# Two modulation chunks moved into the first full gate tile, and the finish of each chunk set ahead of other work

## The chip, the cores and the metric

The kernel runs on one core of a Trainium2 chip. The metric is the device time of one execution in microseconds (us). TensorE (PE) does the matrix products, VectorE (DVE), ScalarE (ACT) and GpSimd (POOL) the elementwise work, and SyncE (SP) issues the loads. Each engine, SP too, works through its own list of instructions in order, so what waits holds up what stands behind it in that list.

## The reference, cut to what matters

A two-layer backbone over 256 latent tokens and 256 context tokens, width 2048, all in float32. Layer 0 mixes by pooling, layer 1 by neighbourhood attention; each layer ends in a gated MLP with a width-3 convolution of the gate (5504 hidden columns). Every sub-layer is modulated by vectors worked out from `silu(c)` and `silu(c_ctx)`:

```python
ml = (silu_c @ w_mod[i] + b_mod[i]).reshape(B, 6, 1, D)       # six vectors of 2048
a_lat = modulate(rms_norm(h, norm1_g[i]), ml[:, 0], ml[:, 1])  # shift, scale of the mixer
h = h + ml[:, 2] * y_lat                                       # gate of the mixer
h = h + ml[:, 5] * conv_ffn(modulate(rms_norm(h, norm2_g[i]), ml[:, 3], ml[:, 4]), ...)
```

The last of the six (`ml[:, 5]`) is only used where the output of the MLP's down product is added to `h`.

## The kernel before, in words

**Products.** A float32 weight is split into a high and a low part (`split`, lines 135 to 151: ACT casts the high part at L147, DVE subtracts at L149), and an activation likewise, and three products hi·hi, hi·lo, lo·hi are summed in PSUM. Each product has 512 columns: 256 of the latent and 256 of the context stream.

**Loads.** `load` (L125) brings weights in pieces of 128 x 1024 values, 512 KB each, into staging slots that `stage` (L115) takes in rotation from the list `rooms`. There are six slots of their own (`wst1` to `wst6`); while the tiles of the activation `A` are not yet written, `lend` adds some of them to the list. A slot can be loaded again when the last instruction that reads its old piece is done: the split for an ordinary weight, the product itself for a modulation weight, which is used unsplit. After layer 0's partial sums `rooms` is cut to slots 1, 2 and 3 (L670, L671), because slots 4 to 6 serve layer 1's modulation weights (`mod_pairs`).

**Modulation of layer 0.** The six vectors are made in 24 chunks of 512 columns (chunk 4w+q is quarter q of vector w; chunks 20 to 23 are the MLP's output gate). `mod_pe` (L195) does one chunk in four steps, one step for each 512 rows of `w_mod`: two loads of 512 KB and eight small products into the PSUM bank "m" (L206); I call such a step a quarter, 22.0 for step 0 of chunk 22, and 22.0a and 22.0b its two loads (columns 0 to 1023 and 1024 to 2047 of the piece). After the fourth step ACT copies the bank to SBUF (L219, `modev`), PE transposes it (L224, `modt`, at high priority), DVE sums the four row groups (L226) and `finish_mod` adds the bias (L189). These last parts run when the generator is asked for the following step. `need(n)` (L487) runs steps until n are done, 96 and an end in all. `shifts(g)` (L470) copies the finished shift vector of group g to where PE multiplies it by the weights (L583).

**Stages of layer 0.** After the mixer of group g, `partial(g)` (L565) multiplies group g (512 of 2048 rows) of the MLP's first eight gate and up tiles (`cg`, `cu`), and the function `between` (L640), called 32 times in each `partial`, asks for modulation steps at a set rate. In `partial(3)` it also normalises the tiles A0 to A11 for the remaining gate tiles and starts the gates 0 to 3. Then come gate 6, A12 to A15, and `gu0(8)`: the first gate and up tile over the whole width (96 products `g`, `u`, L687 to L689). `down0(0)` follows (L697): the down product of hidden tiles 0 to 3, 16 output tiles of 12 products each (`d`, L713 to L715), for which `wd` is loaded in eight pieces. Each output tile is scaled by the output gate (L725) and added to `h` by GpSimd. From there PE goes on with gate tiles and down products without a break to the end of the layer.

**Order.** The program is written in one sequence; a scheduler sets each engine's order by a simulated timeline and by priority, and `tc.high_priority()` puts what is inside it ahead of other work that is ready. PSUM banks: four for `gu`, three for `d`, one for `m`. `bank` (L71) can place every fourth "d" tile in "m" once `nbank[0]` is set, which happens when all modulation steps are done (L662, L663):

```python
            need(97)
            nbank[0] = 0
            A.update(F)
```

Of the kernel before, what the change touches and what calls it, by code (L numbers as in the profile page):

```python
# [13 lines left out]
ALU = mybir.AluOpType  # L14
AX = mybir.AxisListType
# [15 lines left out]
NS = 8  # L31
NC = 6

LEAD = 18
RATE = 20
PMAX = 30

NRH = 3
GATES = (16, 19, 22, 25)
# [20 lines left out]
def kernel(ctx: ExitStack, tc: tile.TileContext, xT, cxT, wmod, wg, wu, wd, wp,  # L60
                         wq, wv, wo, vec, cc, rope, inv, strips, out):
    nc = tc.nc
# [6 lines left out]
    nbank = [None]  # L69

    def bank(tag, name):  # L71

        if tag == "d" and nbank[0] is not None:
            nbank[0] += 1
            if nbank[0] % 4 == 0:
                tag = "m"
        return pp.tile([P, 512], F32, tag=tag, bufs={"gu": 4, "d": 3, "m": 1}[tag], name=name)
# [8 lines left out]
    def V(name):  # L86
        a, b = _OFF[name]
        return vt[:, a:b]
# [22 lines left out]
    def lend(ks):  # L111

        rooms[:] = [r for r in rooms if r < 0 or r in ks] + [k for k in ks if k not in rooms]
# [11 lines left out]
    def load(src, cols, name):  # L125

        ts = []
        for j in range(0, cols, 1024):
            n = min(1024, cols - j)
            t = stage(f"{name}_{j}")  # L130
            fetched.append(nc.sync.dma_start(t[:, :n], src(j, j + n)).ins)
            ts.append((t, n))
        return ts
# [19 lines left out]
    def ld(src, name, share=0):  # L153
        return split(load(lambda a, b: src[:, a:b], 2048, name), name, share)


    modT = {}

    both = (0, 1)

    def mod_tile(l, ch):

        return main.tile([P, 4, 2], F32, tag=f"modT{ch if ch < 20 else (l, ch)}", name=f"modT{l}_{ch}")

    def by_row(ps):

        return ps.rearrange("p (i j c) -> p i c j", i=4, j=4)[:, :, 0:2, :]
# [9 lines left out]
    def finish_mod(l, ch, streams, src):  # L177

        mt = src[0] if len(src) == 1 else mod_tile(l, ch)
        n = len(streams)  # L180
        which, q = divmod(ch, 4)

        def dup(name, a):
            return V(name)[:, a : a + 8].rearrange("p (i s) -> p i s", s=2)[:, :, 0:n]

        bias = dup(f"bm_{l}", 8 * ch)
        for b, v in enumerate(src):
            own = slice(32 * b, 32 * b + 32) if len(src) > 1 else slice(0, P)
            nc.vector.tensor_tensor(mt[own, :, 0:n], v, bias[own], op=ALU.add)  # L189
        if which in (1, 4):  # L190
            nc.vector.scalar_tensor_tensor(mt[:, :, 0:n], mt[:, :, 0:n], 1.0, dup(f"g{1 if which == 1 else 2}_{l}", 8 * q),
                                           op0=ALU.add, op1=ALU.mult)
        modT[l, ch] = mt

    def mod_pe(l, ch, sc, pool):  # L195

        ps = bank("m", f"mod{l}_{ch}")
        held = []
        for g in range(4):
            ts = load(lambda a, b: wmod[l, ch, g, :, a:b], 2048, f"wm{l}_{ch}_{g}")  # L200
            held.append((g, ts, fetched[-2:]))
            if ch > 20 or g % 2:
                with ExitStack() as behind:
                    for n, (gg, tt, _) in enumerate(held[::-1]):
                        for j in (2, 3, 0, 1):
                            ins = nc.tensor.matmul(ps[32 * j : 32 * j + 32, :], sc[:, 4 * gg + j, :],  # L206
                                                   tt[j // 2][0][:, 512 * (j % 2) : 512 * (j % 2) + 512],
                                                   start=(g < 2 and (n == 0 and held[0][0] == 0)),
                                                   stop=(g == 3 and gg == held[0][0]), tile_position=(0, 32 * j))
                            if n == 0 and j == 2:  # L210
                                for x in sum((d for _, _, d in held), []):
                                    tc.add_manual_dep(ins.ins, x.name, mybir.DependencyInfo(
                                        mybir.DependencyClass.Sync, mybir.DependencyReason.DATA), reason="whole")
                                behind.enter_context(tc.issue_after(ins.ins))
                                behind.enter_context(tc.high_priority())
                held = []
            if g == 3:
                ev = pool.tile([P, 512], F32, tag="t2", name=f"modev{l}_{ch}")
                nc.scalar.copy(ev, ps)  # L219
            yield  # L220
        with tc.high_priority():
            p2 = bank("d", f"modt{l}_{ch}")
            for i in range(4):
                nc.tensor.transpose(p2[:, P * i : P * i + P], ev[:, P * i : P * i + P], ident)  # L224
        r = mod_tile(l, ch)
        nc.vector.tensor_reduce(out=r, in_=by_row(p2), axis=AX.X, op=ALU.add)  # L226
        finish_mod(l, ch, both, [r])

    def mod_pairs(todo, ring):

# [143 lines left out]
    chunks = [list(range(f, min(f + 4, NF))) for f in range(0, NF, 4)]  # L374
# [3 lines left out]
    with ExitStack() as ph0:  # L378
# [58 lines left out]
        acts = {}  # L437
# [3 lines left out]
        with ExitStack() as phs:  # L441
# [20 lines left out]
            shs = []  # L462
# [6 lines left out]

            def shifts(g):  # L470
                READY.add(g)
                nc.vector.tensor_copy(shs[g % 2][:, :, 0:2], modT[0, 12 + g])

            def mods():

# [9 lines left out]
            done = [0]  # L485

            def need(n):  # L487
                while done[0] < n:
                    next(pump0, None)
                    done[0] += 1  # L490
# [140 lines left out]
            for g in range(4):  # L631
                if g < 3:
                    lend((range(8, KT), [*range(12, KT), *range(4)], range(8))[g])
                mix = mixer(g + 1) if g < 3 else None
                todo = [20 * g + 20 + n for n in STEPS] if g < 3 else []
                last = [14]
                F = {}
                rstd = n2.acc

                def between(half):  # L640
                    need(min(20 * g + LEAD + RATE * (half + 1) // 32, 20 * g + LEAD + PMAX))
                    if (g, half) in LENT:
                        lend(LENT[g, half])
                    if g == 3 and half == NRH:
                        nc.scalar.copy(rstd, n2.rstd())
                        late_norm.append(rstd)
                    if todo and done[0] > todo[0] and half >= last[0] + 2:
                        last[0] = half
                        todo.pop(0)
                        next(mix)  # L650
                    k = (half - NRH) // 2
                    if g == 3 and 0 <= k < 12 and (half - NRH) % 2 == 0:
                        normalise(0, 3, h_of, both, rstd, f0, range(k, k + 1), keep=F)
                    if g == 3 and half in GATES:
                        e = GATES.index(half)
                        acts[e], _ = gate0(e, *late(e))

                partial(g, shs[g % 2], between)
                for n in todo:
                    need(n)  # L660
                    next(mix)
            need(97)  # L662
            nbank[0] = 0  # L663
            A.update(F)

        whx = ph0.enter_context(tc.tile_pool(name="whx", bufs=1, reuse_waits="tile"))
# [6 lines left out]
        one = [(1, q, 2, (0,)) for q in range(8, 24, 2)]  # L673
        pump = mod_pairs([x for t in zip(two, one) for x in t], ring)

        def gu0(f):
            res = []
            for nm, wsrc in (("g", wg), ("u", wu)):
                parts = ld(wsrc[0, f], f"w{nm}0_{f}")
                if f > NS + 3:  # L680
                    next(pump, None)
                ps = bank("gu", f"{nm}0_{f}")
                for k in range(KT):
                    hi, lo = parts[k // 8]
                    c = P * (k % 8)
                    xh, xl = flat(A[k][:, 0]), flat(A[k][:, 1])
                    nc.tensor.matmul(ps, hi[:, c : c + P], xh, start=(k == 0), stop=False)  # L687
                    nc.tensor.matmul(ps, hi[:, c : c + P], xl, start=False, stop=False)  # L688
                    nc.tensor.matmul(ps, lo[:, c : c + P], xh, start=False, stop=(k == KT - 1))  # L689
                    if k == 7 and f > NS + 3:  # L690
                        next(pump, None)
                res.append(ps)
            return res

# [36 lines left out]
        normalise(0, 3, h_of, both, rstd, f0, range(12, 14))  # L731
        acts[NC], sg = gate0(NC, *r6)
        normalise(0, 3, h_of, both, rstd, f0, range(14, KT))
        res = gu0(NS)
        rest = [e for e in range(NS) if e not in acts]

        def more():
            e = rest.pop(0) if rest else None
            if e is not None:
                acts[e], _ = gate0(e, *late(e))  # L740

        while rest and rest[0] < 4:
            more()
        down0(0, chunks[0], [acts[f] for f in chunks[0]], more)
        while rest:
            more()
        acts[NS], sg = gate0(NS, *res)
# [42 lines left out]
    with ExitStack() as ph2:  # L790
# [164 lines left out]
        for c, fs in enumerate(chunks):  # L955
            acts = []
# [404 lines left out]
```

## Time and profile before

| what | value |
|---|---|
| median of 3 executions | 3050.64 us (3046.84 to 3052.1) |
| the profiled execution | 3052.48 us, its span 3050.7 us |
| PE busy | 2976.8 us, 98% of the span |
| DVE, ACT, POOL busy | 64%, 45%, 28% |
| mean DMA rate | 184 GB/s |
| mean granted TensorE clock | 0.992 |

A row of the timeline reads: start, duration, engine, line, operation, output <- inputs, shape, count; in brackets the idle time of the engine before it and what ended it. Names lose their numbers, so `mod<-wm` is any modulation product and `cu<-Ad` any partial up product; `SPq` rows are load issues. A row of the waits reads: who, for what; us in total, times, longest. A row of the stages reads: stage, its length, then busy us and count of each engine, granted clock of PE, DMA share, GB/s. A row of the DMA issues ends with the median us from the issue to the landing.

### The profile page before, as it was taken

To read this page: it belongs to the slowest core of one execution; us is meant where nothing else is said; L and a number is where in the kernel's file an instruction comes from. 1 tells how busy PE (TensorE), PEld (TensorE's weight loads), DVE (VectorE), ACT (ScalarE), POOL (GpSimd) and SP (SyncE) were. 2 spreads that over 40 slices of the span, in tenths; PEclk is the share of its full clock that TensorE was granted. 3 is DMA by queue.
4 is the path that set the end of the run, shared out by engine and by line. 5 is a ranking of instruction groups with operands and counts; after the bars stand their busy time and mean duration, and the time that the engine had idled before them with its cause. 6 is when DMAs were issued, how large, how long until landed. Compare 5 with 4: busy or idle time off the path is not lost.

```text
span 3050.7 us, 40962 instructions
## 1 busy us (share of the span) xinstructions
PE 2976.8 (98%) x15092; PEld 2416.8 (79%) x15092; DVE 1949.0 (64%) x2765; ACT 1377.7 (45%) x2237; POOL 849.4 (28%) x840
## 2 busy tenths in 40 slices
PE   5999999999999999999999999999999999999998
PEld 2666668888888888888887888878788888888887
DVE  4455764386574857658485666474778666666666
ACT  4333454323333242333334444343556666666665
POOL 2111313303122030311312001020002566566665
PEclk9999999999999999999999999999999999999999
DMA  9888663384665747566482333343346655555563
GB/s 392 328 305 313 218 208 98 104 255 142 216 189 170 235 149 237 154 205 211 148 256 75 114 108 110 110 128 103 110 155 194 192 187 193 189 184 187 183 198 110
DMA packets 178503, 561.80 MB, mean 184 GB/s; under 512 B 17664, under 2 KB 22272, under 8 KB 178304
## 3 DMA queue, kind: packets, MB, share of 16 engines
q1 hardware_dynamic: 178304, 559.19, 56.2%
q8 instruction: 119, 1.95, 0.2%
q14 instruction: 80, 0.66, 0.1%
HBM read 557.03 MB, written 2.10 MB: 183 GB/s over the span
## 4 chain that ended last, share of the span: by engine, by line
PE 91%; DMA 3%; DVE 3%; POOL 1%; issue 1%; ACT 1%; SPq 0%; DVEq 0%; POOLq 0%; ACTq 0%
PE g L882 5%; PE u L882 5%; PE d L713 5%; PE d L714 5%; PE d L715 5%; PE d L935 4%; PE g L687 4%; PE g L689 4%; PE g L688 4%; PE u L688 4%; PE u L689 4%; PE u L687 4%; PE g L885 3%; PE u L885 3%; PE d L939 2%; PE mod L206 2%
## 5 line engine op out<-in xcount | busy, mean ns | idle before, releaser
L726 POOL TENSOR_TENSOR hl<-hl,dy 128x256 f32<-128x256 f32 x160 | 146.3, 914 | 942.1 <-ACT dy L725 941.9
L950 POOL TENSOR_TENSOR hl<-hl,dy 128x256 f32<-128x256 f32 x320 | 332.1, 1074 | 188.3 <-ACT dy L948 186.0
L262 DVE SCALAR_TENSOR_TENSOR macc<-wm,sc,macc 128x512 f32<-128x512 f32 (+1 forms) x360 | 328.8, 944 | 67.5 <-DMA wm<-wmod 66.7
L725 ACT ACTIVATE dy<-d,modT 128x256 f32<-128x256 f32 x320 | 133.0, 469 | 187.7 <-PE d L715 171.8
L726 POOL TENSOR_TENSOR hc<-hc,dy 128x256 f32<-128x256 f32 x160 | 129.5, 809 | 0.0
L948 ACT ACTIVATE dy<-d,modT 128x512 f32<-128x512 f32 x160 | 104.6, 684 | 42.9 <-PE d L939 41.3
L149 DVE TENSOR_TENSOR wd_2l<-wd,wd_2h 128x1024 fp32r<-128x1024 f32 (+1 forms) x44 | 54.6, 1246 | 108.2 <-ACT wd_2h L147 106.9
L206 PE MATMUL mod<-wm,sc 128*32 128x512 f32 x768 | 98.3, 633 | 9.7 <-DMA wm<-wmod 8.1
L1037 POOL TENSOR_TENSOR rk<-rk,rp 128x256 f32<-128x256 f32 x16 | 15.1, 944 | 330.6 <-DVE rk L1036 237.5
L149 DVE TENSOR_TENSOR wd_3l<-wd,wd_3h 128x1024 fp32r<-128x1024 f32 (+1 forms) x44 | 52.0, 1202 | 77.9 <-ACT wd_3h L147 76.5
L149 DVE TENSOR_TENSOR wd_1l<-wd,wd_1h 128x1024 fp32r<-128x1024 f32 (+1 forms) x44 | 53.7, 1224 | 60.8 <-ACT wd_1h L147 60.8
L521 POOL TENSOR_TENSOR pf<-ws,inv 128x256 f32<-128x256 f32 x32 | 29.4, 939 | 212.2 <-DVE ws L516 149.8
L147 ACT CAST wd_1h<-wd 128x1024 fp32r<-128x1024 f32 (+1 forms) x44 | 45.3, 1032 | 81.4 <-PE u L688 56.9
L149 DVE TENSOR_TENSOR wd_0l<-wd,wd_0h 128x1024 fp32r<-128x1024 f32 (+1 forms) x44 | 54.5, 1247 | 37.3 <-ACT wd_0h L147 37.3
L147 ACT CAST wd_0h<-wd 128x1024 fp32r<-128x1024 f32 (+1 forms) x44 | 45.2, 1032 | 56.0 <-PE u L882 29.1
L1126 ACT ACTIVATE sb<-sb,nm 128x512 f32<-128x512 f32 x64 | 46.1, 721 | 52.7 <-DVE nm L1122 52.2
L914 DVE TENSOR_TENSOR actb<-sgb,actb 128x256 fp32r<-128x256 f32 x43 | 51.4, 1195 | 26.0 <-ACT actb L913 26.0
L206 PEld LDWEIGHTS mod<-wm,sc 128*32 128x32 f32 x768 | 21.7, 113 | 57.8 <-issue 55.1
L713 PE MATMUL d<-act,wd_2h 128*128 128x512 f32 x172 | 67.1, 390 | 0.0
L715 PE MATMUL d<-act,wd_2l 128*128 128x512 f32 x172 | 66.9, 389 | 0.0
L714 PE MATMUL d<-act,wd_2h 128*128 128x512 f32 x172 | 66.9, 389 | 0.0
L715 PE MATMUL d<-act,wd_0l 128*128 128x512 f32 x172 | 66.9, 389 | 0.0
(1750 smaller groups left out, 9312.7 us busy)
## 6 DMA issues: line engine op xcount, KB each, us to landing
wm<-wmod SPq DMA_DIRECT2D x384, 512.0 KB, 6.1
wd<-wd SPq DMA_DIRECT2D x168, 512.0 KB, 4.5
wg<-wg SPq DMA_DIRECT2D x156, 512.0 KB, 4.6
wu<-wu SPq DMA_DIRECT2D x156, 512.0 KB, 4.6
wv<-wv SPq DMA_DIRECT2D x32, 512.0 KB, 4.2
wk<-wq SPq DMA_DIRECT2D x32, 512.0 KB, 4.1
wq<-wq SPq DMA_DIRECT2D x32, 512.0 KB, 4.0
wo<-wo SPq DMA_DIRECT2D x32, 512.0 KB, 4.4
```

What stands on the lines that cost most here:

```text
L149: eng.tensor_tensor(lo[:, :n], t[:, :n], hi[:, :n].bitcast(F32), op=ALU.subtract)
L262: nc.vector.scalar_tensor_tensor(acc[s], v, sc2[:, k, s : s + 1], acc[s], op0=ALU.mult, op1=ALU.add)
L687: nc.tensor.matmul(ps, hi[:, c : c + P], xh, start=(k == 0), stop=False)
L688: nc.tensor.matmul(ps, hi[:, c : c + P], xl, start=False, stop=False)
L689: nc.tensor.matmul(ps, lo[:, c : c + P], xh, start=False, stop=(k == KT - 1))
L713: nc.tensor.matmul(ps, hi[:, o : o + P], xh, start=(i == 0), stop=False)
L714: nc.tensor.matmul(ps, hi[:, o : o + P], xl, start=False, stop=False)
L715: nc.tensor.matmul(ps, lo[:, o : o + P], xh, start=False, stop=(i == n - 1))
L726: nc.gpsimd.tensor_tensor(h_of(s)[:, k, :], h_of(s)[:, k, :], y[:, s], op=ALU.add)
L882: nc.tensor.matmul(ps, hi[:, c : c + P], flat(B[k]), start=(k == 0), stop=False)
L885: nc.tensor.matmul(ps[:, T:], lo[:, c : c + P], B[k][:, 0], start=False, stop=(k == KT - 1))
L950: nc.gpsimd.tensor_tensor(hl[:, k, :], hl[:, k, :], y[:, q], op=ALU.add)
```

## The change

- In `mod_pe` ACT's copy `modev` and DVE's sum and `finish_mod` go under `tc.high_priority()`, and so does the copy in `shifts`.
- A constant `LAST = 88` stops the modulation steps in `partial(3)` after 22 of the 24 chunks. The remaining eight steps (chunks 22 and 23) run inside `gu0(8)`: after every fourth of the 16 row tiles of g and of u one step is asked for. The end of chunk 23 (transpose, sum, bias) is asked for after the first four output tiles of `down0(0)`, and only there `nbank[0]` is set.

```diff
             if g == 3:
                 ev = pool.tile([P, 512], F32, tag="t2", name=f"modev{l}_{ch}")
-                nc.scalar.copy(ev, ps)
+                with tc.high_priority():
+                    nc.scalar.copy(ev, ps)
...
-        r = mod_tile(l, ch)
-        nc.vector.tensor_reduce(out=r, in_=by_row(p2), axis=AX.X, op=ALU.add)
-        finish_mod(l, ch, both, [r])
+            r = mod_tile(l, ch)
+            nc.vector.tensor_reduce(out=r, in_=by_row(p2), axis=AX.X, op=ALU.add)
+            finish_mod(l, ch, both, [r])
...
-                nc.vector.tensor_copy(shs[g % 2][:, :, 0:2], modT[0, 12 + g])
+                with tc.high_priority():
+                    nc.vector.tensor_copy(shs[g % 2][:, :, 0:2], modT[0, 12 + g])
...
-                    need(min(20 * g + LEAD + RATE * (half + 1) // 32, 20 * g + LEAD + PMAX))
+                    need(min(20 * g + LEAD + RATE * (half + 1) // 32, 20 * g + LEAD + PMAX, LAST))
...
-            need(97)
-            nbank[0] = 0
+            need(LAST)
             A.update(F)
...
-        def gu0(f):
+        def gu0(f, aside=None):
...
                     if k == 7 and f > NS + 3:
                         next(pump, None)
+                    if k % 4 == 3 and aside is not None:
+                        aside()
...
-        res = gu0(NS)
+        res = gu0(NS, lambda: need(done[0] + 1))
...
-        down0(0, chunks[0], [acts[f] for f in chunks[0]], more)
+        def more_and_mods():
+            need(97)
+            nbank[0] = nbank[0] or 0
+            more()
+
+        down0(0, chunks[0], [acts[f] for f in chunks[0]], more_and_mods)
```

Since `stage` hands out slots in the order in which the program is written, the 16 loads of chunks 22 and 23 now come after the cut of `rooms`: they share slots 1, 2 and 3 with the loads of `gu0(8)` and `down0(0)`. In the order that the scheduler sets for the changed kernel, the first instruction that stands elsewhere is, on SP, the one after the loads of the last `cg` weights; up to there, which is up to about 375 us of the profile, all five engines have the same order as before.

More of the change, by code (lines that the diff above doesn't have):

```diff
@@ L36 @@
 PMAX = 30
+LAST = 88
 NRH = 3
```

## The prediction

> **What bounds the kernel now.** I read the page first:
>
> ```profile
> span 3050.7 us, 40962 instructions
> PE 2976.8 (98%) x15092; PEld 2416.8 (79%) x15092; DVE 1949.0 (64%) x2765; ACT 1377.7 (45%) x2237; POOL 849.4 (28%) x840
> ```
>
> PE is the bound, so a change that neither adds nor removes products moves the time by PE's idle time, and by its clock. The change touches the end of the pooling stage up to the first down product. The stage view there:
>
> ```profile
> 372.00:400.00 28.00, 25.52 (x143) 14.84 (x141) 19.76 (x38) 13.29 (x26) 6.41 (x4) 1.00 0.92 306
> 400.00:424.90 24.90, 20.41 (x112) 12.43 (x112) 18.40 (x32) 14.45 (x23) 2.76 (x2) 0.93 0.72 250
> 424.90:448.40 23.50, 23.50 (x96) 19.27 (x97) 14.18 (x26) 11.54 (x23) 0.00 (x0) 0.93 0.44 148
> 448.40:492.00 43.60, 43.60 (x194) 36.10 (x193) 20.91 (x22) 27.23 (x52) 25.71 (x30) 1.00 0.28 88
> ```
>
> PE idles 7.0 us between 372 and 424.9, and not at all from there on: a delay at 448 has nothing behind it that would absorb it. PE's waits in this stretch, then two of the whole run:
>
> ```profile
> PE cu L600 <- ACT wcu_4h L147: 3.4, 1, 3.4
> PE g L687 <- DVE late L410: 2.1, 1, 2.1
> PE mod L206 <- DMA wm<-wmod: 1.2, 1, 1.2
> PE modt L224 <- ACT modev L219: 0.3, 1, 0.3
> ...
> PE modt L224 <- ACT modev L219: 9.6, 8, 3.1
> PE pwg L583 <- DVE sh L472: 3.4, 1, 3.4
> ```
>
> The first four are the 7.0. The 3.4 is for the last `cu` weights, whose loads stand behind ten of chunks 22 and 23. Idle time also costs clock: after the wait that ends at 424.90, ten products in 3.4 us at clock 0.50, then sixteen at 1.00.
>
> ```profile
> 424.90 0.50 PE L687 MATMUL g<-A,wg_8h 128*128 128x512 f32 x1 [2.12 <-DVE late L410]
> 426.30:429.70 3.40, 3.40 (x10) 2.62 (x9) 3.40 (x7) 3.40 (x9) 0.00 (x0) 0.50 0.97 352
> 430.00:433.40 3.40, 3.40 (x16) 2.79 (x16) 3.40 (x9) 2.56 (x5) 0.00 (x0) 1.00 0.33 128
> 402.40:405.80 3.40, 3.40 (x16) 1.73 (x14) 2.72 (x6) 0.87 (x3) 0.00 (x0) 0.50 0.05 18
> ```
>
> At half clock, 3.4 us lose 1.7. The stretch has two such dips, 3.4 together, so what the change can win here is 7.0 + 3.4 = 10.4 us.
>
> **Part 1, the finish ahead of other work.** The 9.6 and 3.4 above are what it aims at. But up to the last `cg` loads the changed kernel's instructions stand in the old order on all five engines: the finish of chunks 0 to 20 already stood first. I take 0 for it; its bounds are the 13.0 us of these waits as a gain, and, the order being the same, no loss. The sums of chunks 21 to 23 are needed only by the down product's scaling.
>
> **Part 2, the two chunks moved.** Prices:
>
> ```profile
> L713 PE MATMUL d<-act,wd_0h x172: 389/389/390, 448.4 to 1636.4; 128*128 128x512 f32 x172
> L713 PE MATMUL d<-act,wd_2h x172: 388/389/478, 470.2 to 1655.4; 128*128 128x512 f32 x172
> 383.36 1.06 PE L206 MATMUL mod<-wm,sc 128*32 128x512 f32 x8 [1.22 <-DMA wm<-wmod]
> 422.18 0.60 PE L616 MATMUL ptu<-ident,peu 128*128 128x128 f32 x4
> 379.92 1.09 PE L583 MATMUL pwg<-wcg,sh 128*32 128x256 f32 x16
> 384.31:424.77 40.46, 34.85 (x188) 21.34 (x184) 31.54 (x60) 24.16 (x45) 5.70 (x4) 0.96 0.78 266
> 344.94 1.78 SPq L131 DMA_DIRECT2D wm<-wmod  x4
> wm<-wmod SPq DMA_DIRECT2D x1, 512.0 KB, 4.1
> wm<-wmod SPq DMA_DIRECT2D x1, 512.0 KB, 5.0
> wm<-wmod SPq DMA_DIRECT2D x1, 512.0 KB, 5.8
> wd<-wd SPq DMA_DIRECT2D x1, 512.0 KB, 3.5
> wu<-wu SPq DMA_DIRECT2D x1, 512.0 KB, 4.0
> ```
>
> The first 96 down products take 470.2 - 448.4 = 21.8 us, 0.227 each; a quarter takes 1.06, a transposition 0.60, `pwg` or `pwu` 1.09; DVE's 60 rows from 384.31 on take 0.53 each. The 4.1, 5.0 and 5.8 are the first three of the four loads issued together from 344.94 on, 0.45 apart: they land 4.1, 5.4 and 6.7 after the first issue. Single loads of `wd` and `wu` took 3.5 and 4.0.
>
> When a slot is free, the next load goes at once:
>
> ```profile
> 378.34 1.07 PE L206 MATMUL mod<-wm,sc 128*32 128x512 f32 x8
> 379.43 1.60 SPq L131 DMA_DIRECT2D wm<-wmod  x2
> 417.84 1.23 DVE L149 TENSOR_TENSOR wg_8l<-wg,wg_8h 128x1024 fp32r<-128x1024 f32 x1 [3.31 <-ACT wg_8h L147]
> 419.09 0.33 SPq L131 DMA_DIRECT2D wu<-wu  x1
> 423.17 1.04 ACT L147 CAST wu_8h<-wu 128x1024 fp32r<-128x1024 f32 x1 [0.59 <-DMA wu<-wu]
> SPq L131 <- PE mod L206: 54.0, 13, 8.1
> ```
>
> A quarter ends at 379.41, its slots are loaded from 379.43; a split ends at 419.07, its slot's load goes at 419.09. The last row (SP's own waits, 330 to 480) says that SP already waits for quarters to free slots, 54.0 us. With six slots and lent tiles that runs ahead of PE. In the changed kernel 16 modulation loads, 2 of `wu` and 8 of `wd` go through three slots (the 2 of `wg` come before), and with the loads set in SP's list as they are, each must wait for a product just ahead of its own use. I walk PE along its new order, on the old clock:
>
> 1. The `cg` and `cu` products run without quarters between: 92 left from 381.98 at 0.227 are 20.9, plus a transposition and the 1.1 of `pwu`: 404.6. The `cu` loads take the place of 22.0's in SP's list, 17.5 us earlier, so the 3.4 goes. Late next is DVE: the last `cu` tile, which PE reaches at 401.9, needs a bank that DVE frees with the sum of `ptg` (L623), in its new list behind 34 instructions from 384.31 on: 17.9, and I add 1.1 for waits on ACT: 403.3. **Idle 1.4.** End 406.0; quarter 22.0, loaded in time, ends at 407.1.
> 2. Both loads of 22.1 stand on SP behind 22.2a, which takes the slot of 22.0b. So they go when quarter 22.0 ends, as second and third of a train: 407.1 + 6.7 = 413.8. PE has only two transpositions meanwhile, to 408.3: **idle 5.5**. This also covers the 2.1 for `late`, 50 instructions down DVE's list: 384.3 + 26.3 = 410.6, with the waits for ACT, one of them for a cast that must wait for the end of `cu`, about 413.4. Quarter 22.1 ends at 414.9.
> 3. 36 `g` products, 8.2, with a dip, 1.6: 424.7. Quarter 22.2 ends at 425.8; 12 products to 428.5. The first half of `wu` takes the slot of 22.2b: issue 425.8, 4.0 to land, 1.05 cast: 431.0. **Idle 2.4.**
> 4. Two `u` products, quarter 22.3, dip: 433.3. It frees the slot of the second half of `wu`, third in its train: 440.0, cast 441.1, low part 442.3. PE's 22 products, a transposition and quarter 23.0 last to 441.0: **idle 1.0**. 24 products: 447.4.
> 5. 23.1a is third in its train behind the split of `wu`, 0.3 late: quarter to 448.7. 23.2b takes the slot of 23.1a, second in its train: 448.8 + 5.4 = 454.2. Nothing stands between: **idle 5.5**. Quarter 23.2 with part of a dip: 455.8.
> 6. The first `wd` half takes the slot of 23.2b: 455.8 + 3.8 + 1.05 = 460.7. **Idle 4.9.** The down product starts at 460.7 instead of 448.4.
> 7. Behind it the second `wd` pair goes only after quarter 23.3: dip 1.7, waits of 1.8 and 0.75. The first 96 down products end after 21.8 + 1.1 + 0.6 + 4.2 = 27.7, at 488.4 instead of 470.2.
>
> That is 18.2 later. As a check by sums: new idle 1.4 + 5.5 + 2.4 + 1.0 + 0.3 + 5.5 + 4.9 + 2.5 = 23.5, new dips 1.6 + 1.6 + 0.5 + 1.7 = 5.4, less 10.4: 18.5. I take 18.3. Bounds: five turns with the 3.5 of `wd` in place of 4.1 and no new dip give 18.3 - 3.0 - 5.4 = +10. At the other end the rate of the busy queue:
>
> ```profile
> wm<-wmod SPq DMA_DIRECT2D x19, 512.0 KB, 7.0
> ```
>
> With 7.0 instead of 4.1, five turns cost 14.5 more: +33. I hold to 4.1, since the landing rows above come from stretches in which one to four loads were under way, as here.
>
> [...]
>
> The rest of part 2 costs nothing: the bank "m" for every fourth down tile comes four tiles later, while ACT empties a bank in under 1 us and one is filled in 12 x 0.227 = 2.7. GpSimd's list is the same. At the start of layer 1 a few `v` products swap places; the stretch has 5 us of idle:
>
> ```profile
> 1664.00:1680.00 16.00, 10.92 (x32) 7.73 (x33) 9.08 (x25) 5.07 (x13) 1.02 (x1) 0.57 0.01 5
> ```
>
> I take 0, with 1 us to either side.
>
> **The rivals.** *The loads come in time (faster).* If the turn of a slot were shorter than PE's work up to the next use, all four waits and both dips go: 3050.6 - 10.4 = 3040. It decides at a turn of about 1.2 us in step 2 and 0 in steps 5 and 6. That the last waits are for weights standing behind modulation loads speaks for it; every landing row speaks against it. [...]
>
> *The turns are half hidden (no change).* PE would have waited for DVE anyway: its rows are busy 31.5 of these 40.5 us, and the change squeezes the same normalising and gates into less time. But DVE only bears on steps 1 to 3; with these free, 18.3 - 5.5 - 2.4 - 1.6 = +8.8, 3059. It takes steps 5 and 6 at half price too, about -5: 3054, within 0.2%.
>
> *The queue is busy and every wait brings a full dip (slower still).* One busy landing of 7.0 in each turn: 3050.6 + 33 = 3084.
>
> **How the numbers follow.** The profiled execution took 3052.5 (1.8 around the span), 1.8 above the median; the added waits do not depend on that, so I add 18.3 to the median: 3069. Chances: the forecast, +10 to +26, 0.75; slower still 0.11; half hidden 0.06; faster 0.08. The range 3058 to 3079 leaves out the faster and half-hidden cases and most of the slowest. 0.2%, 6 us, is about what a measurement of this kernel tells from no change: faster 0.08, same 0.05, slower 0.87.
>
> **What would show it.** In the profile after: the 3.4 for `wcu_4h` and the 2.1 for `late` gone; PE waits of `mod L206` for DMA `wm` of about 5 us, twice, around 408 and 449; `u` and `d` waiting for ACT's casts of `wu_8h` (2 to 3) and `wd_0h` (about 5), after SP waits on `mod L206`; the down product starting near 461; the clock at 0.50 after each; and the stretch after 490 as before. A down product starting before 450 proves the walk wrong; if it starts at 461 and the total is lower, the delay was absorbed later. Most uncertain is the sum of the turns: SP's list is certain, the landing times are not.

## The result, and the profile after

The changed kernel takes 3077.67 us (median of 4 executions, 3071.86 to 3080.71) against 3049.78 (3046.84 to 3052.1): ratio 1.009, 95% interval 1.0077 to 1.0103. It is slower, as forecast; the predicted 3069 is 8.7 below the median, which is inside the predicted range. The profiled execution took 3071.86, its span is 3070.1.

The page of the changed kernel:

```profile
span 3070.1 us, 40956 instructions
PE 2978.0 (97%) x15092; PEld 2415.3 (79%) x15092; DVE 1951.6 (64%) x2765; ACT 1377.8 (45%) x2237; POOL 851.2 (28%) x840
```

PE has as many products as before and is busy 1.2 us longer; nearly all of the 19.4 us that the span has grown is idle. The stages, with the columns of the stage view before and one stage more:

```profile
372.00:400.00 28.00, 27.29 (x151) 19.51 (x150) 23.03 (x35) 16.95 (x30) 6.43 (x4) 1.00 0.62 210
400.00:424.90 24.90, 17.49 (x84) 11.49 (x82) 23.38 (x48) 16.39 (x34) 2.91 (x2) 0.86 0.39 120
424.90:448.40 23.50, 19.67 (x88) 12.24 (x88) 2.81 (x4) 2.67 (x3) 0.00 (x0) 0.93 0.52 179
448.40:492.00 43.60, 30.53 (x128) 21.25 (x121) 12.47 (x13) 15.13 (x24) 9.68 (x12) 0.80 0.45 145
492.00:600.00 108.00, 108.00 (x479) 89.41 (x478) 45.23 (x47) 46.26 (x77) 33.04 (x35) 1.00 0.32 98
```

From 400 to 492 PE is idle for 7.4 + 3.8 + 13.1 = 24.3 us, and its mean clock is 0.86, 0.93 and 0.80, where it was 0.93, 0.93 and 1.00; from 492 on it is full again at clock 1.00. So the loss is made in this stretch and kept to the end. PE's waits in it (372 to 500):

```profile
PE mod L207 <- DMA wm<-wmod: 13.5, 3, 7.4
PE d L717 <- ACT wd_0h L148: 5.0, 1, 5.0
PE u L689 <- ACT wu_8h L148: 2.9, 2, 2.2
PE d L717 <- ACT wd_1h L148: 1.8, 1, 1.8
PE cu L605 <- DVE wcu_4l L150: 0.7, 1, 0.7
PE u L691 <- DVE wu_8l L150: 0.5, 1, 0.5
PE d L719 <- DVE wd_1l L150: 0.5, 1, 0.5
```

The 3.4 for `wcu_4h` and the 2.1 for `late` are gone; in their place PE waits for the moved modulation weights and for `wu` and `wd`, which share three slots with them. Where these waits stand (timeline of PE; in the order: last `pwg` products, quarters 22.0, 22.1 and 22.2, first `u`, quarters 23.1 and 23.2, first `d`, first `d` of the second pair, 97th `d`):

```profile
377.80 1.09 PE L586 MATMUL pwg<-wcg,sh 128*32 128x256 f32 x16
...
403.51 1.06 PE L207 MATMUL mod<-wm,sc 128*32 128x512 f32 x8
...
413.01 1.93 PE L207 MATMUL mod<-wm,sc 128*32 128x512 f32 x8 [7.41 <-DMA wm<-wmod]
...
424.25 1.07 PE L207 MATMUL mod<-wm,sc 128*32 128x512 f32 x8
...
430.44 0.62 PE L689 MATMUL u<-A,wu_8h 128*128 128x512 f32 x1 [2.17 <-ACT wu_8h L148]
...
448.08 1.07 PE L207 MATMUL mod<-wm,sc 128*32 128x512 f32 x8 [0.39 <-DMA wm<-wmod]
454.89 1.94 PE L207 MATMUL mod<-wm,sc 128*32 128x512 f32 x8 [5.74 <-DMA wm<-wmod]
461.78 0.79 PE L717 MATMUL d<-act,wd_0h 128*128 128x512 f32 x1 [4.95 <-ACT wd_0h L148]
...
470.58 0.50 PE L717 MATMUL d<-act,wd_1h 128*128 128x512 f32 x1 [1.85 <-ACT wd_1h L148]
...
491.19 0.39 PE L717 MATMUL d<-act,wd_2h 128*128 128x512 f32 x1
```

SP's own waits from 400 to 475, the two longest:

```profile
SPq L132 <- DMA wm<-wmod: 31.5, 7, 5.7
SPq L132 <- PE mod L207: 20.7, 8, 4.9
```

SP waits for the earlier load of a slot to land, and then for the quarter that reads it: 22.0b, issued at 397.93, landed 4.3 later, but 22.2a, which takes its slot, went at 404.60, when quarter 22.0 had ended.

A quarter of 1.93 or 1.94 instead of 1.06 ran at half clock. The granted clock is 0.50 for 6.83 us from 410.20, 3.41 from 430.69, 13.65 from 451.17 and 3.41 from 471.64.

For the comparisons below I use one length, **S**: from the last of the `pwg` products (0.71 behind the start of the row that groups its sixteen, so 380.63 before and 378.51 after) to the first `d` of the third `wd` pair (48 products use one pair of pieces), the 97th down product. Before, S is 470.18 - 380.63 = 89.55; after, 491.19 - 378.51 = 112.68. From that product to the first product of the normalisation behind layer 0 the profile before takes 1194.84 us and the one after 1194.85, so what S loses is lost for good. Ahead of it and in layer 1 the executions scatter by up to 5 us: between the two profiles, S is 23.1 longer, the start 2.1 shorter, layer 1 and the last normalisation 1.6 shorter, together the 19.4 between the spans.

### The profile page after: what moved, and what is told of

Its sections match the earlier page's. It is cut to its first block, busy times and chain, and to the rows that moved or that the text cites. A ratio compares the mean times of both kernels' runs of the same rounds, so it can differ in the third digit from the quotient of the medians.

```text
span 3070.1 us, 40956 instructions
## 1 busy us (share of the span) xinstructions
PE 2978.0 (97%) x15092; PEld 2415.3 (79%) x15092; DVE 1951.6 (64%) x2765; ACT 1377.8 (45%) x2237; POOL 851.2 (28%) x840
## 4 chain that ended last, share of the span: by engine, by line
PE 91%; DMA 3%; DVE 3%; POOL 1%; ACT 1%; issue 1%; SPq 0%; DVEq 0%; ACTq 0%; POOLq 0%
PE d L717 5%; PE g L891 5%; PE u L891 5%; PE d L718 5%; PE d L719 5%; PE d L944 4%; PE g L689 4%; PE g L691 4%; PE g L690 4%; PE u L689 4%; PE u L690 4%; PE u L691 4%; PE u L894 3%; PE g L894 3%; PE mod L207 2%; PE d L948 2%
## 5 line engine op out<-in xcount | busy, mean ns | idle before, releaser
L207 PE MATMUL mod<-wm,sc 128*32 128x512 f32 x768 | 99.4, 639 | 23.1 <-DMA wm<-wmod 22.9
L717 PE MATMUL d<-act,wd_0h 128*128 128x512 f32 x172 | 68.3, 397 | 5.0 <-ACT wd_0h L148 5.0
L717 PE MATMUL d<-act,wd_1h 128*128 128x512 f32 x172 | 67.4, 392 | 1.8 <-ACT wd_1h L148 1.8
L719 PE MATMUL d<-act,wd_1l 128*128 128x512 f32 x172 | 67.6, 393 | 0.5 <-DVE wd_1l L150 0.5
L718 PE MATMUL d<-act,wd_0h 128*128 128x512 f32 x172 | 67.9, 395 | 0.0
```

The costliest lines, as they stand in the source:

```text
L717: nc.tensor.matmul(ps, hi[:, o : o + P], xh, start=(i == 0), stop=False)
L718: nc.tensor.matmul(ps, hi[:, o : o + P], xl, start=False, stop=False)
L719: nc.tensor.matmul(ps, lo[:, o : o + P], xh, start=False, stop=(i == n - 1))
```

## The experiments

My theory: part 1 is worth nothing, and part 2 costs because 26 loads now go through three slots, each load waiting for a product that stands just ahead of its own use. The rivals: the moving itself costs (quarters among gate products, a denser DVE); or the half clock behind the waits is the greater part.

| kernel | median us | ratio to before (95%) | S in its profile |
|---|---|---|---|
| before | 3047.4 to 3049.8 in five measurements | 1 | 89.55 |
| part 1 alone | 3046.50 | 0.9997 (0.9988 to 1.0006) | 84.63 |
| before, six slots | 3046.85 | 0.9996 (0.9987 to 1.0005) | 86.55 |
| changed, again | 3073.13 | 1.0080 (1.0067 to 1.0094) | 112.45 |
| part 2 alone | 3074.99 | 1.0087 (1.0072 to 1.0102) | 112.96 |
| changed, one chunk moved | 3058.09 | 1.0032 (1.0019 to 1.0045) | 96.46 |
| changed, six slots | 3046.08 | 0.9989 (0.9979 to 0.9998) | 85.49 |
| six steps moved, six slots | 3051.09 | 1.0011 (1.0002 to 1.0020) | 89.03 |
| four steps, six slots | 3042.59 | 0.9985 (0.9975 to 0.9994) | 83.46 |
| three steps, six slots | 3042.65 | 0.9982 (0.9973 to 0.9991) | 82.45 |
| two steps, six slots | 3045.52 | 0.9993 (0.9984 to 1.0002) | 85.28 |
| changed, zeros 48, 40, 24 | 3074.87 | 1.0090 (1.0076 to 1.0104) | 114.47 |
| changed, zeros 28, 24, 16 | 3072.96 | 1.0090 (1.0078 to 1.0103) | 112.00 |

### Which part costs

Part 2 alone, the changed kernel without the three high-priority edits:

```diff
                 ev = pool.tile([P, 512], F32, tag="t2", name=f"modev{l}_{ch}")
-                with tc.high_priority():
-                    nc.scalar.copy(ev, ps)
+                nc.scalar.copy(ev, ps)
...
-                with tc.high_priority():
-                    nc.vector.tensor_copy(shs[g % 2][:, :, 0:2], modT[0, 12 + g])
+                nc.vector.tensor_copy(shs[g % 2][:, :, 0:2], modT[0, 12 + g])
```

> Part 2 alone: the two chunks are moved, and the three high-priority edits are undone. Its five engine lists are those of the changed kernel, so by my theory (part 1 is worth nothing, all of the loss is part 2) it takes what the changed kernel takes, 3072 to 3081 us, ratio to the kernel before 1.007 to 1.011, and PE waits about 7.4 for a modulation load near 413, 5.7 near 455 and 5.0 for the cast of the first wd near 462. Rival: part 1 carries a cost or a gain of its own that the list of instructions does not show; then the ratio leaves 1.0077 to 1.0103.

It took 3074.29 to 3075.45, with waits of 6.9, 6.1 and 4.8 at the three places. The changed kernel, measured again with a second profile, took 3073.13. The three profiles of this order agree in S to 0.5 (112.45, 112.68, 112.96). Part 1 alone keeps those edits and undoes the move:

```diff
-                    need(min(20 * g + LEAD + RATE * (half + 1) // 32, 20 * g + LEAD + PMAX, LAST))
+                    need(min(20 * g + LEAD + RATE * (half + 1) // 32, 20 * g + LEAD + PMAX))
...
-            need(LAST)
+            need(97)
+            nbank[0] = 0
...
-        res = gu0(NS, lambda: need(done[0] + 1))
+        res = gu0(NS)
...
-        down0(0, chunks[0], [acts[f] for f in chunks[0]], more_and_mods)
+        down0(0, chunks[0], [acts[f] for f in chunks[0]], more)
```

> Part 1 alone: the high-priority edits, no chunk moved. Its five lists are those of the kernel before. Theory (part 1 is worth nothing): ratio 0.999 to 1.001, the stretch from the last pwg product to the 97th down product 89.5 within 1 us, and the waits for modev (9.6) and sh (3.4) as before. By theory A of the run above its profiled execution is shorter than the 3052.5 of the profile before, 3045 to 3050. Rival (the edits were aimed at 13 us of waits): faster by 5 to 13.

It took what the kernel before takes, within 0.12% by the interval. Its waits in the whole run (first two rows) and from 372 to 500 (the rest):

```profile
PE modt L226 <- ACT modev L221: 11.5, 7, 5.2
...
PE pwg L586 <- DVE sh L475: 3.4, 1, 3.4
...
PE g L690 <- DVE late L412: 2.6, 1, 2.6
PE cu L603 <- ACT wcu_4h L148: 1.9, 1, 1.9
PE mod L207 <- DMA wm<-wmod: 0.9, 1, 0.9
```

The waits that part 1 aims at are still there. All of the loss is part 2. One part of the expectation missed: S is 84.63, not 89.5, though the list of every engine is that of the kernel before. Here the waits in the stretch are 5.4 us, where the profile before had 7.0, and no stretch at half clock follows them; that profile had two of 3.41.

### Slots, or the move itself

The changed kernel, in which the rotation is cut to three slots only behind the first down product:

```diff
         ring = range(NW // 2 + 1, NW + 1)
-        rooms[:] = [r for r in rooms if -r not in ring]
...
         down0(0, chunks[0], [acts[f] for f in chunks[0]], more_and_mods)
+        rooms[:] = [r for r in rooms if -r not in ring]
```

> The changed kernel, with the rotation of staging slots cut from six to three only behind down0(0), so that the moved loads, those of wu and those of wd have six slots. Theory (turns of three slots): each load goes before the product ahead of its use has run, so the waits at quarters 22.1 and 23.2, at wu and at wd go, with at most one of 4 to 5 us left where a slot waits for a cast that stands behind the cu products; 3040 to 3056 us, ratio 0.997 to 1.002. Rival 1 (the move itself: modulation quarters between gate products, a denser DVE and ACT, other DMA traffic): the loss stays, 3066 us or more, ratio 1.005 or more, with PE waiting for DVE or ACT instead. Rival 2 (half clock is the greater part): the waits go but dips of 3.4 us multiples stay, ratio about 1.004.

S falls from 112.7 to 85.49 and the ratio to 0.9989. Two rows of its stage view, and its only row of PE waits from 372 to 500:

```profile
424.90:448.40 23.50, 23.50 (x118) 15.77 (x117) 8.91 (x15) 7.30 (x12) 0.00 (x0) 1.00 0.60 199
448.40:492.00 43.60, 43.60 (x196) 36.13 (x195) 24.80 (x25) 28.40 (x54) 27.98 (x31) 1.00 0.37 127
```
```profile
PE mod L207 <- DMA wm<-wmod: 5.0, 2, 4.7
```

Two chunks are still moved, six of the eight quarters still stand behind the last `cu` products, and PE no longer idles from 424.9 on. (Quarters 22.0 and 22.1 are set earlier, since their loads come earlier.) The one long wait left, 4.7 at quarter 22.2, is the one that was expected. The rival that the move itself costs falls. This run alone doesn't hold the order still: PE's list differs from that of the changed kernel from quarter 22.0 on. That the loads were held by slots is read from SP's waits in the changed kernel, above. The kernel before with the same edit, and no move:

> The kernel before with the rotation cut to three slots only behind down0(0): do the extra slots alone change the time, without any move? By my theory PE waits for no load after 400 in the kernel before, so they are worth nothing there: ratio 0.999 to 1.001, the 3.4 for wcu and 2.1 for late still there. Rival (the gain of the six-slot versions came from slots, not from the move): ratio 0.997 to 0.999.

0.9996 (0.9987 to 1.0005): without the move, the slots are worth nothing that can be told from noise. So the slots matter to the moved loads.

### The dose

The changed kernel with `LAST = 92`, still three slots: only chunk 23 is moved.

```diff
-LAST = 88
+LAST = 92
```

> The changed kernel with LAST = 92: only chunk 23 is moved, still through three slots. Theory (turns): the four moved quarters keep the waits at 23.2 and at the two pairs of wd (together about 5.5 + 5 + 2.4) and lose those around 22.1 and at wu; about half to two thirds of the loss, 3060 to 3070 us, ratio 1.003 to 1.007, and the down product starts at about 454 to 458. Rival (a fixed cost of running quarters inside the gate tile, or of the late end of chunk 23): the ratio stays at 1.008 or more. Rival (PE would have waited for DVE anyway): 1.000 to 1.002.

The ratio is at the lower edge of what was expected, and the down product started at 450.3, earlier than 454. Its waits (372 to 500):

```profile
PE u L689 <- ACT wu_8h L148: 5.5, 2, 5.0
PE mod L207 <- DMA wm<-wmod: 3.4, 2, 2.1
PE g L689 <- DVE late L412: 3.2, 1, 3.2
```

They are turns of slots again, but at `wu` rather than at `wd`: with four quarters less, all moved ones are over before `wd` comes.

### What the half clock costs

Products by a zero matrix, added to the bank that is being summed, keep PE busy in the three longest waits and leave the loads as they are:

```diff
+FILL = {(22, 0): 12, (23, 1): 10, (23, 2): 6}
...
+                for n in range(4 * FILL.get((ch, g), 0)):
+                    j = n % 4
+                    nc.tensor.matmul(ps[32 * j : 32 * j + 32, :], zero, hl[:, 0:2, :].rearrange("p s t -> p (s t)"),
+                                     start=False, stop=False, tile_position=(0, 32 * j))
```

> The changed kernel with products by a zero matrix into the bank that is being summed, which PE does in the three longest waits: 48 after quarter 22.0, 40 after quarter 23.1, 24 after quarter 23.2. The result is the same, the loads and their slots are untouched, so the turns stay and only the half clock behind the waits can go. From the profile after, work done at half clock is about 4.0 behind the wait of 7.4, 1.9 behind that of 5.7, 3.0 behind that of 4.9, half of which is lost: 2.0 + 1.0 + 1.5 = 4.5 us less than the changed kernel, 3069 to 3073, the dips at 410 and 451 gone or shorter and the 97th down product 3 to 5 earlier. Rival (the half clock is the greater part of the loss): 10 us or more less. Rival (PE busy with zeros delays the quarters): the same or slower than the changed kernel.

48 of these took 10.5 us and 40 took 8.8, 0.218 each, so they ended behind the loads: S 114.47. With 28, 24 and 16:

> The run with zero products again, with fewer of them: there one took 0.218 instead of the 0.133 of a modulation product, and 48 and 40 of them ended 2 to 3 us behind the landing of the loads. Now 28, 24 and 16, which are 6.1, 5.2 and 3.5 us in waits of 7.4, 5.7 and 4.9. The order in the stretch is that of the changed kernel but for the zeros. Theory (the half clock is a small term): the windows at 410 and 451 gone, the 97th down product 3 to 5 us earlier after the last pwg than the 112.5 of the changed kernel, and 3 to 5 less in the median, 3068 to 3071. Rival (the half clock is most of the loss): 10 less or more.

Now they fit, and the long half-clock windows are gone: 0.50 is granted only for 3.41 from 433.33 and 6.83 from 470.88. Yet S is 112.00, 0.5 to 1.0 shorter than in the three profiles with the same loads and no zeros, not 3 to 5. Its waits (372 to 500):

```profile
PE d L728 <- ACT wd_1h L151: 2.9, 1, 2.9
PE mod L210 <- DMA wm<-wmod: 2.6, 3, 1.1
PE u L700 <- ACT wu_8h L151: 2.4, 2, 2.1
PE g L700 <- DVE late L423: 1.8, 1, 1.8
PE d L728 <- ACT wd_0h L151: 1.4, 1, 1.4
```

What quarter 22.1 gains by the full clock PE spends waiting for `late`, which had been hidden; and the wait for the second `wd` pair is 2.9 instead of 1.9, with 6.83 at half clock behind it instead of 3.41. The half clock is not what the loss is made of: in this run 9.7 us of PE's work in S stand at half clock, which loses 4.8, against 3.4 in the profile before, and S is still 22 us longer than there. Taking away one delay uncovers the next.

### How many steps to move

Given six slots, moving fewer steps beats the kernel before. `LAST = 92`, with the edit of the six-slot version:

> LAST = 92 and the rotation cut to three slots only behind down0(0). Theory (turns): four moved quarters whose eight loads have six slots; no wait for a modulation load, for wu or for wd above 2 us, the old 3.4 for wcu and 2.1 for late gone or halved; 3040 to 3051 us, ratio 0.997 to 1.000, the down product at 440 to 449. Rival 1 (the move itself costs): 1.004 or more.

3042.59, with two waits left, 0.9 for a modulation load and 1.9 for `late`. Six steps and two steps:

> LAST = 90 with six slots: six steps moved. Theory: between the versions with 88 (0.9989) and 92 (0.9985), unless one load again takes a slot whose reader stands behind the cu products, as in the version with 88 (4.7 at quarter 22.2): 3040 to 3047, ratio 0.997 to 1.000; quarters 22.2 to 23.3 stand among the g and u products, so the wait for late stays or grows by up to 2.

> LAST = 94 with six slots: only the last two steps of chunk 23 are moved behind the partial sums. In its list quarters 23.2 and 23.3 stand right ahead of the first g product, where the version with LAST = 92 still had the wait of 1.9 for late and a half-clock window. Theory (with slots enough, a moved quarter only fills time in which PE waits): that wait gone or under 1, no half-clock window there, but more of the old waits at the cu weights, whose loads again stand behind two more modulation loads; 3040 to 3046, ratio 0.997 to 0.9995. Rival (fewer moved, less gained): as the kernel before, 0.999 to 1.001.

Six steps missed: 1.0011. Loads cost it only 1.1, but the transposition of chunk 23 waits 2.8 for `modev` right ahead of the first down product, and `late` takes 2.6:

```profile
PE modt L226 <- ACT modev L221: 2.8, 1, 2.8
PE g L688 <- DVE late L412: 2.6, 1, 2.6
```

Two steps keep a wait of 3.0 for `wcu_4h`, and their 0.9993 can't be told from the kernel before. Three steps:

> LAST = 93 with six slots: quarter 23.0 stays among the partial sums, so only one pair of modulation loads more than with 92 stands ahead of the last cu loads, and quarters 23.1 and 23.2 stand right ahead of the first g product. Theory: the wait for late (1.9 with 92) goes, the wait for the cu weights (3.0 with 94) is 0 to 2; 3040 to 3045, ratio 0.9975 to 0.999, the stretch from the last pwg to the 97th down product 81 to 84. Rival (each version between 88 and 96 trades one wait for another): 0.999 to 1.000, as with 94.

```profile
PE cu L603 <- ACT wcu_4h L148: 2.1, 1, 2.1
PE mod L207 <- DMA wm<-wmod: 1.4, 1, 1.4
```

0.9982, S 82.45; with four steps, whose interval overlaps, the fastest here: 5 to 6 us under the kernel before.

## Why the prediction was right, and where it was not

**Part 1 is worth nothing.** Right, and shown to about 0.1%.

**The walk through the slots.** Right in its mechanism: every wait that it named occurred but one, all but one of these for the named reason, and with more slots only one long wait of this kind was left. Set on the clock of the profile before (after's times plus 2.12), the starts are:

| | predicted | measured |
|---|---|---|
| 22.1 | 413.8 | 415.1 |
| 22.2 | 424.7 | 426.4 |
| first `u` | 431.0 | 432.6 |
| 23.2 | 454.2 | 457.0 |
| first `d` | 460.7 | 463.9 |
| 97th `d` | 488.4 | 493.3 |

*Step 1* had an idle of 1.4 for a bank that DVE frees; it was 0.7, for another reason.

*Step 2* named the wrong releaser. The pair of 22.1 was to go when quarter 22.0 ends, 0.45 apart from 22.2a. But 22.1a takes the slot of the second `wg` half, whose cast stands behind the end of `cu`: DVE's split of it ended at 405.14 + 1.22 = 406.36, and the load went at 406.38, 1.8 behind 22.2a (issues of SP, the split on DVE, and SP's own wait for it):

```profile
404.60 0.33 SPq L132 DMA_DIRECT2D wm<-wmod  x1
```
```profile
405.14 1.22 DVE L150 TENSOR_TENSOR wg_8l<-wg,wg_8h 128x1024 fp32r<-128x1024 f32 x1
```
```profile
406.38 0.33 SPq L132 DMA_DIRECT2D wm<-wmod  x1
```
```profile
SPq L132 <- DVE wg_8l L150: 1.4, 1, 1.4
```

I had that cast in step 2, but only as a reason for `late`. This is 1.3 of the 4.9.

*Steps 3 to 6* add another 1.9, in pieces of -0.1 to 0.6. The landings held: the pair for 23.2 landed 5.7 after its first issue (5.4 predicted), the second half of `wu` 6.7 after the first issue of its train (6.7 predicted). More of it is half clock that I counted too low: quarter 23.2 took 1.94 where I had 1.6, and the two `u` products with quarter 22.3 took 2.8 where I had 2.3.

*Step 7* is off by 1.7. I counted one dip of 1.7; the window of 13.65 us also reaches over the first 3 us of down products, another 1.5.

By sums: idle time in S rose from 6.97 to 25.03, by 18.1 (predicted 23.5 - 7.0 = 16.5). Of the 27.3 us at half clock, 11.7 are idle, so 15.6 of work lose 7.8, 4.4 more than before (predicted 5.4 - 3.4 = 2.0). Together 22.5 of the 23.1.

**The other term that failed is the 10.4 taken off**, and with it the sentence that the added waits do not depend on the execution. The 7.0 of waits and two dips of the stretch before are one execution's. With the same order on every engine, part 1 alone shows 5.4 of waits and no dip; the six-slot version of before, whose lists differ only from 409 on and not on PE, shows 5.8 and one. What the change removes from those two is 5.4 and 7.5, not 10.4, and S after is longer than those two by 112.7 - 84.6 = 28.1 and 112.7 - 86.6 = 26.1. So against part 1 alone the forecast of 18.2 is some 10 too low, half of it by the walk's 4.9 and half by this term. The medians say the same: 27.9, 24.8 and 26.9 in the three measurements with this order. That the two profiled executions differ by 19.4, close to the predicted 18.3, is chance: 23.1 in the stretch less 3.7 of scatter elsewhere.

**The rivals.** *The loads come in time*: false with three slots; true in kind with six. *Half hidden*: DVE's `late` does stand close behind, 1.8 by the run with zeros; there it absorbed what the full clock gained, while the turns of the slots cost more than predicted, not less. *A busy queue, 7.0 a landing*: the loads of these turns took 3.5 to 6.1, the 6.1 as third of a train.

Left open: three executions of the first measurement took 3076 to 3081, where the later ones of the same order took 3070 to 3075.5. None of the three has a profile. Two of the five executions with 28, 24 and 16 zeros also took 3078 and 3081.

## What to carry to other kernels

When work with loads is moved, walk its loads through the slots that they get at the new place: the loss here came from a cut of the slot list that happens to stand ahead of the new place, and moving the cut, not the work, turned 1.009 into 0.999. Look for the last reader of each slot on every engine, since a split far down another list can hold a load longer than the product in view, as the one of step 2 did by 1.8. And what a change can win must not be read from one execution: the same lists gave 5.4 to 7.0 us of waits in one stretch, and none to two stretches of 3.41 us at half clock behind them.

## What was not expected of the hardware

In the profiles before and after, the clock is granted at 0.50 in 17 stretches. The last of each profile aside, they took 3.41 us (9 times), 6.83 (3 times) or 13.65 (3 times).

The longer of two waits for the same tile was the one without half clock behind it. The kernel before and part 1 alone waited for `late` (a row of the stages, the wait in part 1 alone, and two more rows of the stages):

```profile
422.88:426.29 3.41, 1.39 (x6) 1.17 (x7) 3.38 (x10) 2.35 (x4) 0.00 (x0) 1.00 0.81 243
```
```profile
421.00 0.50 PE L690 MATMUL g<-A,wg_8h 128*128 128x512 f32 x1 [2.59 <-DVE late L412]
```
```profile
416.42:419.83 3.41, 1.99 (x13) 1.38 (x11) 3.01 (x2) 1.79 (x3) 1.30 (x1) 1.00 0.67 229
419.83:423.24 3.41, 2.24 (x10) 1.87 (x11) 3.38 (x12) 3.21 (x6) 0.00 (x0) 1.00 0.92 318
```

Before, the wait of 2.12 ended at 424.90: PE was busy for 1.39 of the 3.41 us up to 426.29, and for the 3.41 behind that the clock was granted at 0.50. In part 1 alone the wait of 2.59 ended at 421.00: PE was busy for 1.99 and 2.24 of the two stretches of 3.41 that it lies in, and the clock was 1.00 in both and stayed there up to 492. What decides between the two is not shown here. PE's ends are modelled in the profile, so its busy times are only as sharp as that.
